# Two of four pairs of up chunks, in the second to fourth round of both MLPs, by seven products in place of eight

## Chip, cores and metric

The kernel runs on one core of one Trainium2 chip. The metric is the device time of one execution in microseconds (us). A core has the engines TensorE (PE; its weight loads are shown as PEld), VectorE (DVE), ScalarE (ACT) and GpSimd (POOL), and the queue SyncE (SP), which here issues the transfers.

## The reference

One inference step of a two-layer decoder over 512 prompt rows and 8 x 8 sample rows, 576 rows in all, with a model width of 1024. The change lies in the MLPs, one in each layer:

```python
def rmsnorm(x, g):
    y = x32 * lax.rsqrt(jnp.mean(x32 * x32, axis=-1, keepdims=True) + RMS_EPS)
    return (y * g.astype(jnp.float32)).astype(x.dtype)

def sqrelu_mlp(h, w_up, w_down):
    return jnp.square(jax.nn.relu(h @ w_up)) @ w_down

for l in range(DEPTH):
    ...
    hp = hp + sqrelu_mlp(rmsnorm(hp, norm_mlp[l]), mlp_w_up[l], mlp_w_down[l])
    hs = hs + sqrelu_mlp(rmsnorm(hs, norm_mlp[l]), mlp_w_up[l], mlp_w_down[l])
```

`w_up` is 1024 x 4096 and `w_down` 4096 x 1024, all in float32. The mixers (retention with gMLP, then attention) are not touched.

## The kernel before

Everything is held transposed: width on the 128 partitions, the 576 rows along the free axis, as two halves of 288 (`TH`). `h[0..7]` are the eight chunks of the residual stream. Each float32 product is made of three: both operands are split into a high part (`hi`, a cast on ACT) and a low part (`lo`, a subtraction on DVE), and PE adds hi x hi, hi x lo and lo x hi. For the norm's output these are `norm.xs[c]` (tiles xhi and xlo); for the weights they are `whi` and `wlo`, each 128 x 512, made in `prepare` (L272) and `split_low` (L283) with `NW_` = 6 buffers.

An MLP runs in four rounds of `rounds_of`. In a round, four pairs of **up chunks** come first. An up chunk (`up`, through `block`, L328) is 128 columns of `w_up`: eight blocks of the contraction, times three parts, times two halves, 48 products into one `acc` tile of two PSUM banks. Then DVE takes it out with relu and the norm's factor (tile `t`, L490), ACT squares it (tile `q`, L495), and once both chunks of a pair are there, four DVE passes over 288 columns (L503 to L506) make combinations, ACT casts them in two goes (`ahi`, L498) and DVE makes the low parts (`alo`, L499).

Four **down units** of `down_unit` follow. Each makes two row chunks and two halves from a 2 x 2 block product with seven products for eight (P1 to P7; L340 in `product`), where `q`'s combinations are the right operands, and combinations of weight blocks (`total`, L257: the sums s1 to s4, one DVE pass of 128 x 512 each) are among the left ones. Seven products of 12 matmuls stand in a unit. Results that take part in several outputs are carried on by ACT copies inside PSUM (`y`, `z`, `w`), between products that don't need them; in down units 1 to 3, P5 goes into a tile `f` of its own.

The order on DVE and ACT inside an MLP is the order of the code (`manual_schedule`). `jobs` lists which weight half or combination comes when; `ahead_to` prepares jobs some places ahead of PE, and `load_free` starts the transfer of the next `raw` weight tile (512 KB, three buffers; during the down units a fourth in the buffer of `q`) once a tile has been used up.

Of the kernel before, what the change touches and what calls it, by code (L numbers as in the profile page):

```python
# [11 lines left out]
F32 = mybir.dt.float32  # L12
F32R = mybir.dt.float32r
AF = mybir.ActivationFunctionType
ALU = mybir.AluOpType
# [3 lines left out]
P = 128  # L19
D = 1024  # L20
KC = D // P
NP = 512
NS = 64
T = NP + NS
TH = T // 2
# [5 lines left out]
FB = 8  # L31
# [10 lines left out]
NW_ = 6  # L42
# [70 lines left out]
NCOL = 59  # L113
UNIT = ("P1", "P5", "P6", "P2", "P7", "P3", "P4")
SUMS = {"P1": "s1", "P5": "s2", "P2": "s3", "P6": "s4"}
FIRST_UNIT = ("P1", "P2", "P3", "P5", "P6", "P4", "P7")


@with_exitstack
def hybrid_step(ctx: ExitStack, tc: tile.TileContext, a, o):  # L120
    nc = tc.nc
# [17 lines left out]
    def ks(name, dt=F32):  # L139
# [8 lines left out]
    cols = keep.tile([P, NCOL], F32, name="cols")  # L148
# [67 lines left out]
    used, done, summed = [0], [0], [0]  # L216
# [107 lines left out]
    def block(outs, w, x, sides, start, stop):  # L324

        for si, (w_, x_) in enumerate(((w[0], x[0]), (w[0], x[1]), (w[1], x[0]))):
            for hf, out in zip(sides, outs):
                nc.tensor.matmul(out, lhsT=w_, rhs=x_[:, hf if isinstance(hf, slice) else half(hf)],  # L328
                                 start=(start and si == 0), stop=(stop and si == 2))
# [13 lines left out]
    def cut(piece, k):  # L343
        return [w[:, (k % 4) * P:(k % 4 + 1) * P] for w in piece[k // 4]]
# [118 lines left out]

    def rounds_of(norm, nxt, mp):
        rounds, closing = 32 // FB, Closing(COL["fin"])

        def up():

            acc, got = acc_tile(), take(2)
            for k in range(KC):  # L470
                block([acc[:, hf, 0:TH] for hf in range(2)], cut(got, k), norm.xs[k], (0, 1), k == 0, k == KC - 1)
            ahead_to(used[0] + NW_ - 2)
            return acc[:, :, 0:TH]

        def flat(v):
            return v.rearrange("p a b -> p (a b)")

        for r in range(rounds):
            acts, firsts = [], []
            for p in range(FB // 2):  # L480

                q = mp.tile([P, 8, TH], F32, name="q", tag="q", bufs=1)
                hi = mp.tile([P, 7, TH], F32R, name="ahi", tag="ahi", bufs=FB // 2)
                lo = mp.tile([P, 7, TH], F32R, name="alo", tag="alo", bufs=FB // 2)
                for j in range(2):
# [4 lines left out]
                    nc.vector.scalar_tensor_tensor(out=halves(t), in0=view, scalar=0.0, in1=norm.rv,  # L490
                                                   op0=ALU.max, op1=ALU.mult)
                    if p == FB // 2 - 1 and j == 1:
                        ahead_to(used[0] + NW_ - 1)
                    seg = slice(2 * j, 2 * j + 2)
                    nc.scalar.activation(out=flat(q[:, seg]), in_=t, func=AF.Square)  # L495

                def two(s0, s1):
                    nc.scalar.copy(out=hi[:, s0 - 1:s1 - 1], in_=q[:, s0:s1])  # L498
                    nc.vector.tensor_tensor(out=lo[:, s0 - 1:s1 - 1], in0=q[:, s0:s1],  # L499
                                            in1=hi.bitcast(F32)[:, s0 - 1:s1 - 1], op=ALU.subtract)  # L500

                b12, b11, b22, b21, t1, t2, t3, t4 = (q[:, i] for i in range(8))
                nc.vector.tensor_tensor(out=t1, in0=b11, in1=b12, op=ALU.subtract)  # L503
                nc.vector.scalar_tensor_tensor(out=t2, in0=t1, scalar=-1.0, in1=b22, op0=ALU.mult, op1=ALU.subtract)
                nc.vector.tensor_tensor(out=t3, in0=b22, in1=b12, op=ALU.subtract)
                nc.vector.scalar_tensor_tensor(out=t4, in0=t2, scalar=-1.0, in1=b21, op0=ALU.mult, op1=ALU.subtract)  # L506
# [838 lines left out]
def layouts(i):  # L1345


    def chunks(w):

        r, c = w.shape  # L1350
        return w.reshape(r // P, P, c // P, P).transpose(2, 1, 0, 3)

    def down(w):

        return w.reshape(4, 4, 2, P, 4, 2, P).transpose(0, 4, 5, 3, 2, 1, 6).reshape(4, 4, 2, P, 8, P)

    def cols(v):
        return v.reshape(-1, P).T

    x = np.concatenate([i["x_prompt"][0], i["x_sample"].reshape(NS, D)])  # L1360
# [28 lines left out]
        "rot": ROT,  # L1389
    }  # L1390
    for l in range(2):
        out[f"w_up{l}"] = chunks(i["mlp_w_up"][l])
        out[f"w_dn{l}"] = down(i["mlp_w_down"][l])
    return {k: np.ascontiguousarray(v) for k, v in out.items()}


# [20 lines left out]
```

## Time and profile before

| what | value |
|---|---|
| median of 3 runs | 1208.14 us (1206.29 to 1211.4) |
| profiled execution's own time | 1207.19 us |
| its span, first to last instruction | 1205.4 us |
| mean granted clock of TensorE | 0.998 |
| HBM read and written | 102.92 MB and 6.03 MB |
| transfers of up weights | 64 of 512 KB |

The kernel runs mixer 0, MLP 0, mixer 1 and MLP 1. MLP 0's four rounds lie from about 257 us to 640, MLP 1's from about 811 to 1192, and one round takes some 95 us: about 50 for the up chunks, 45 for the down units. Where a line of the profile has a name such as `L328`, that is the line of the code above. "Busy" counts the time in which an engine works on something; a row of idle time names who ended it. The lines of the profile themselves stand in the prediction.

### The profile page before, as it was taken

The numbers are of one execution on the slowest core, as the hardware profiler recorded it, in microseconds if no ns is written. First come the engines' busy times: TensorE is split into PE (matmuls) and PEld (weight loads), VectorE is DVE, ScalarE is ACT, GpSimd is POOL, SyncE is SP. The second block draws the span as 40 slices with busy tenths as digits, with TensorE's granted clock in tenths as the row PEclk, the third lists the DMA queues.
The fourth block names the chain that finished last, engine by engine and source line by source line (L and its number), as shares of the span: only waits on it lengthen the run. The fifth ranks groups of instructions, "written<-read, shape, count | busy, mean of one in ns | idle before, by whom it ended". The sixth has DMA issues, their size and how long they took to land.

```text
span 1205.4 us, 22593 instructions
## 1 busy us (share of the span) xinstructions
PE 1186.1 (98%) x9177; PEld 1169.3 (97%) x9177; DVE 872.6 (72%) x1611; ACT 576.4 (48%) x1082; POOL 157.6 (13%) x137
## 2 busy tenths in 40 slices
PE   8999999999999999999999999999999999999996
PEld 8999999999999999999999999999999999999996
DVE  8977795447866875785797778546785795795696
ACT  6333554444443544453466777444453453453452
POOL 4444250110000000000002654220000000000000
PEclk9999999999999999999999999999999999999999
DMA  7343222222233232232223212122233232232222
GB/s 273 105 141 124 76 76 86 76 66 88 88 105 86 73 122 72 71 107 87 80 84 122 72 38 70 54 75 70 84 96 99 61 115 88 71 106 88 77 82 79
DMA packets 38263, 109.42 MB, mean 91 GB/s; under 512 B 4160, under 2 KB 12544, under 8 KB 38144
## 3 DMA queue, kind: packets, MB, share of 16 engines
q1 hardware_dynamic: 37440, 107.36, 28.8%
q8 instruction: 72, 1.18, 0.4%
q10 hardware_dynamic: 720, 0.62, 0.2%
q14 instruction: 31, 0.25, 0.1%
HBM read 102.92 MB, written 6.03 MB: 90 GB/s over the span
## 4 chain that ended last, share of the span: by engine, by line
PE 82%; DVE 10%; ACT 3%; DMA 3%; issue 2%; SPq 0%; DVEq 0%; ACTq 0%
PE acc L328 54%; PE acc L340 8%; PE f L340 3%; PE y L340 3%; PE w L340 3%; PE z L340 3%; DVE wlo L283 2%; DMA raw<-in_w_dn 2%; ACT s L1101 1%; PE tpp L1161 1%; DVE alo L499 1%; PE op L1176 1%; DVE h L547 1%; PE sp L1142 1%; ACT ahi L498 1%
## 5 line engine op out<-in xcount | busy, mean ns | idle before, releaser
L328 PE MATMUL acc<-xhi,whi 128*128 128x288 f32 x1504 | 321.4, 295 | 0.4 <-DVE vz L765 0.4
L328 PE MATMUL acc<-xhi,wlo 128*128 128x288 f32 x1504 | 319.0, 293 | 0.0
L328 PE MATMUL acc<-xlo,whi 128*128 128x288 f32 x1504 | 318.7, 293 | 0.0
L283 DVE TENSOR_TENSOR wlo<-raw,whi 128x512 fp32r<-128x512 f32 x321 | 232.2, 736 | 76.2 <-ACT whi L272 74.7
L272 ACT CAST whi<-raw 128x512 fp32r<-128x512 f32 x321 | 191.6, 618 | 133.7 <-PE acc L328 100.8
L328 PEld LDWEIGHTS acc<-xhi,whi 128*128 128x128 f32 x1504 | 239.3, 188 | 1.6 <-issue 1.2
L328 PEld LDWEIGHTS acc<-xhi,wlo 128*128 128x128 f32 x1504 | 240.4, 188 | 0.3
L328 PEld LDWEIGHTS acc<-xlo,whi 128*128 128x128 f32 x1504 | 240.0, 188 | 0.0
L495 ACT ACTIVATE q<-t 128x576 f32<-128x576 f32 x64 | 43.9, 686 | 229.5 <-DVE t L490 229.5
L490 DVE SCALAR_TENSOR_TENSOR t<-acc,rstd 128x576 f32<-128x576 f32 x64 | 48.3, 755 | 83.3 <-PE acc L328 82.7
L272 ACT CAST whi<-s 128x512 fp32r<-128x512 f32 x124 | 73.7, 620 | 64.7 <-DVE s L257 55.2
L283 DVE TENSOR_TENSOR wlo<-s,whi 128x512 fp32r<-128x512 f32 x124 | 84.1, 689 | 10.6 <-ACT whi L272 10.6
L499 DVE TENSOR_TENSOR alo<-q,ahi 128x864 fp32r<-128x864 f32 x64 | 77.1, 1205 | 8.3 <-ACT ahi L498 8.3
L498 ACT CAST ahi<-q 128x864 fp32r<-128x864 f32 x64 | 66.5, 1039 | 13.6 <-DVE q L506 12.6
L340 PE MATMUL acc<-ahi,wlo 128*128 128x288 f32 x340 | 71.4, 298 | 0.6
L340 PE MATMUL acc<-ahi,whi 128*128 128x288 f32 x340 | 71.4, 295 | 0.0
L340 PE MATMUL acc<-alo,whi 128*128 128x288 f32 x340 | 70.3, 295 | 0.0
L1046 POOL TENSOR_TENSOR kl<-z,kh 64x512 fp32r<-64x512 f32 x4 | 5.5, 1379 | 394.3 <-ACT kh L1043 394.1
L257 DVE TENSOR_TENSOR s<-raw 128x512 f32<-128x512 f32 x62 | 42.8, 690 | 18.7 <-DMA raw<-in_w_dn 18.7
L340 PEld LDWEIGHTS acc<-ahi,wlo 128*128 128x128 f32 x340 | 53.6, 188 | 2.5 <-DVE wlo L283 2.5
L340 PEld LDWEIGHTS acc<-ahi,whi 128*128 128x128 f32 x340 | 54.0, 188 | 0.0
L340 PEld LDWEIGHTS acc<-alo,whi 128*128 128x128 f32 x340 | 53.7, 188 | 0.0
(331 smaller groups left out, 2109.4 us busy)
## 6 DMA issues: line engine op xcount, KB each, us to landing
raw<-in_w_up SPq DMA_DIRECT2D x64, 512.0 KB
raw<-in_w_dn SPq DMA_DIRECT2D x64, 512.0 KB
raw<-in_w_in SPq DMA_DIRECT2D x22, 512.0 KB
raw<-in_w_o SPq DMA_DIRECT2D x16, 512.0 KB
raw<-in_w_qkv SPq DMA_DIRECT2D x10, 512.0 KB
h<-in_xT SPq DMA_DIRECT2D x8, 288.0 KB
s<-in_s SPq DMA_DIRECT2D x4, 512.0 KB
out_ret_s<-s SPq DMA_DIRECT2D x4, 512.0 KB
```

The costliest lines, as they stand in the source:

```text
L257: nc.vector.tensor_tensor(out=sums[k, i], in0=x, in1=b[y], op=ALU.add)
L272: nc.scalar.copy(out=hi, in_=src)
L283: nc.vector.tensor_tensor(out=lo, in0=src, in1=hi.bitcast(F32), op=ALU.subtract)
L328: nc.tensor.matmul(out, lhsT=w_, rhs=x_[:, hf if isinstance(hf, slice) else half(hf)], start=(start and si == 0), stop=(stop and si == 2))
L340: nc.tensor.matmul(out, lhsT=w[wi][:, k * P:(k + 1) * P], rhs=x(k)[xi], start=(start and n == 0), stop=(stop and n == len(steps) - 1), ski ...
L490: nc.vector.scalar_tensor_tensor(out=halves(t), in0=view, scalar=0.0, in1=norm.rv, op0=ALU.max, op1=ALU.mult)
L495: nc.scalar.activation(out=flat(q[:, seg]), in_=t, func=AF.Square)
L498: nc.scalar.copy(out=hi[:, s0 - 1:s1 - 1], in_=q[:, s0:s1])
L499: nc.vector.tensor_tensor(out=lo[:, s0 - 1:s1 - 1], in0=q[:, s0:s1], in1=hi.bitcast(F32)[:, s0 - 1:s1 - 1], op=ALU.subtract)
L547: nc.vector.tensor_tensor(out=row[:, cols_], in0=row[:, cols_], in1=src, op=op)
L1101: nc.scalar.activation(out=s[:, n, cut_:], in_=s[:, n, cut_:], func=AF.Exp, bias=nm[:, n:n + 1], accum_out=den[:, n:n + 1])
L1142: nc.tensor.matmul(sp[:, i * 256 + 256 - wd:(i + 1) * 256], lhsT=q[kv][:, n * P:(n + 1) * P], rhs=kst[kv][part][:, lo:lo + wd], start=(par ...
```

## The change

In rounds two to four (`r > 0`), the second and the fourth pair of up chunks (`p % 2 == 1`) are made by `up_unit`: a 2 x 2 block product over halves of the contraction, the two chunks, and the two halves of the rows, in seven products of 12 matmuls for eight. The other pairs stay as they are. This needs:

- combinations of the norm's operands (`mix`, called four times in the first round behind up chunks, the places in `MIX`): scaled sums and differences of `h` chunks, split in high and low parts (tiles `xn`), kept through the MLP;
- combinations of up weights, by the same `jobs` and `total` as the down units: four sums and seven splits where a pair had four splits;
- up weights laid out by pairs with the contraction's blocks in another order (`up` in `layouts`), which `up` in `rounds_of` follows;
- DVE writing its result to `q` at once (tile `t` is gone), which ACT squares in place;
- room in SBUF: the DMA scratch is set to 4096.

```diff
+    def in_units(r, p):
+
+        return r > 0 and p % 2 == 1
+
     def mlp_order(l, last):
...
-            add_pieces([up[r * FB + f] for f in range(FB)])
+            for p in range(FB // 2):
+                pair = [up[r * FB // 2 + p, i] for i in range(2)]
+                if in_units(r, p):
+                    add_unit(pair, False)
+                else:
+                    add_pieces(pair)
...
+        def mix(i):
+
+            a, b = 2 * i, 2 * i + 1
...
+            nc.scalar.activation(out=t3, in_=h[a][:, two_], func=AF.Copy, scale=ga)
+            for out, src, g, in1, op in ((t1, h[a][:, one], ga, t3, ALU.subtract), (t3, h[b][:, two_], gb, t3, ALU.subtract),
+                                         (u2, h[b][:, two_], gb, t1, ALU.add), (u4, h[b][:, one], gb, u2, ALU.subtract)):
+                nc.vector.scalar_tensor_tensor(out=out, in0=src, scalar=g, in1=in1, op0=ALU.mult, op1=op)
...
+            for src, sign, hi, lo in zip((t1, u2, t3, u4), (1, -1, 1, -1), his, los):
+                nc.scalar.activation(out=hi, in_=src, func=AF.Copy, scale=float(sign))
+                nc.vector.scalar_tensor_tensor(out=lo, in0=src, scalar=float(sign), in1=hi.bitcast(F32),
+                                               op0=ALU.mult, op1=ALU.subtract)
...
+        def up_unit(q):
+
+            both = acc_tile()
+            x, f = both[:, 0, 0:TH], both[:, 1, 0:TH]
+
+            def run(n, out, start, ahead=NW_ - 1):
+                product(out, take(1)[0], lambda k: [t[operand[n]] for t in mixed[k]], range(4), start, True, True)
+                if ahead:
+                    ahead_to(used[0] + ahead)
+
+            def copied(name, src):
+                out = m_tile(name)[:, 0:TH]
+                nc.scalar.copy(out=out, in_=src)
+                ahead_to(used[0] + NW_ - 1)
+                return out
+
+            def scaled(seg, src, op):
+                nc.vector.scalar_tensor_tensor(out=q[:, seg], in0=src, scalar=0.0, in1=norm.rv[:, seg % 2],
+                                               op0=op, op1=ALU.mult)
+
+            run("P1", x, True, 0)
+            y = copied("y", x)
+            run("P5", f, True)
+            run("P6", x, False, 0)
+            z = copied("z", x)
+
+            nc.scalar.copy(out=q[:, 3], in_=f)
+            run("P2", y, False)
+            scaled(1, y, ALU.max)
+            run("P7", z, False, 0)
+            w_ = copied("w", z)
+
+            nc.vector.tensor_tensor(out=q[:, 2], in0=z, in1=q[:, 3], op=ALU.add)
+            scaled(2, q[:, 2], ALU.min)
+            run("P3", x, False)
+            nc.vector.tensor_tensor(out=q[:, 0], in0=x, in1=q[:, 3], op=ALU.add)
+            scaled(0, q[:, 0], ALU.max)
+            nc.scalar.activation(out=flat(q[:, 0:2]), in_=flat(q[:, 0:2]), func=AF.Square)
+            run("P4", w_, False)
+            scaled(3, w_, ALU.min)
+            nc.scalar.activation(out=flat(q[:, 2:4]), in_=flat(q[:, 2:4]), func=AF.Square)
...
+                if in_units(r, p):
+                    up_unit(q)
+                for j in range(0 if in_units(r, p) else 2):
...
-                    t = mp.tile([P, T], F32, name="t", tag="t")
-                    nc.vector.scalar_tensor_tensor(out=halves(t), in0=view, scalar=0.0, in1=norm.rv,
+                    seg = slice(2 * j, 2 * j + 2)
+                    nc.vector.scalar_tensor_tensor(out=q[:, seg], in0=view, scalar=0.0, in1=norm.rv,
                                                    op0=ALU.max, op1=ALU.mult)
...
+                    if r == 0 and (p, j) in MIX:
+                        mix(MIX.index((p, j)))
```

Three places show how the order of instructions changes. Lines behind the change are some 10 higher up to `add_residual`, and more beyond.

**The second pair of the second round, on ACT and PE.** Before, ACT has behind a pair's second chunk its square (L495), the two casts of the pair (L498), two weight casts (L272) and the next chunk's square:

```order
L495 ACTIVATE q<-t 128x576 [waits DVE_49]
L498 CAST ahi<-q 128x864 [waits Activation_49]
L498 CAST ahi<-q 128x1152 [waits DVE_49]
L272 CAST whi<-raw 128x512 [waits DMAHW7_49,PE_49]
L272 CAST whi<-raw 128x512 [waits PE_49]
L495 ACTIVATE q<-t 128x576 [waits DVE_49,Activation_49]
```

With the change, the same first pair is followed on ACT by the copies of the unit (L525 is `copied`, L539 the copy of f to `q`):

```order
L576 ACTIVATE q<-q 128x576 [waits DVE_49]
L581 CAST ahi<-q 128x864 [waits Activation_49]
L581 CAST ahi<-q 128x1152 [waits DVE_49]
L525 COPY y<-acc 128x288 [waits PE_49]
L282 CAST whi<-s_4341 128x512
L282 CAST whi<-s_4284 128x512
L282 CAST whi<-raw 128x512 [waits DMAHW6_49]
L525 COPY z<-acc 128x288 [waits PE_49]
L282 CAST whi<-raw 128x512 [waits DMAHW7_49]
L539 COPY q<-acc 128x288 [waits DVE_49]
L282 CAST whi<-raw 128x512
L525 COPY w<-z 128x288 [waits PE_49]
```

The copy of y stands right behind the pair's two casts. On PE, the last rows of P1 and the first of P5 of that unit (P5's operand is a combination, `xn`; its result f lies in the same `acc` tile):

```order
L350 MATMUL acc<-xhi,whi 128x288
L350 MATMUL acc<-xhi,wlo 128x288
L350 MATMUL acc<-xlo,whi 128x288
L350 MATMUL acc<-xn,whi 128x288 [waits Activation_49]
L350 MATMUL acc<-xn,wlo 128x288
L350 MATMUL acc<-xn,whi 128x288 x2
```

P5's first matmul waits for ACT, for the count that the copy of y brings; P6 behind it has no wait for ACT of its own.

**The last pair of the second round, on DVE,** from the first chunk's evacuation, or what stands there, to the pair's last low part. Before (L490 takes a chunk out, s are sums of down weights):

```order
L490 SCALAR_TENSOR_TENSOR t<-acc,rstd 128x576
L283 TENSOR_TENSOR wlo<-s_4619,whi 128x512
L283 TENSOR_TENSOR wlo<-s_4536,whi 128x512
L490 SCALAR_TENSOR_TENSOR t<-acc,rstd 128x576
L283 TENSOR_TENSOR wlo<-s_4617,whi 128x512
L503 TENSOR_TENSOR q<-q 128x288
L504 SCALAR_TENSOR_TENSOR q<-q 128x288
L505 TENSOR_TENSOR q<-q 128x288
L506 SCALAR_TENSOR_TENSOR q<-q 128x288
L499 TENSOR_TENSOR alo<-q,ahi 128x864
L499 TENSOR_TENSOR alo<-q,ahi 128x1152
```

With the change, from the last sums of down weights on (L530 is `scaled`, L545 and L548 the additions of f; the four q passes and two alo follow as before):

```order
L267 TENSOR_TENSOR s_5853<-s_5808,raw 128x512
L267 TENSOR_TENSOR s_5855<-s_5853,raw 128x512
L530 SCALAR_TENSOR_TENSOR q<-y,rstd 128x288
L293 TENSOR_TENSOR wlo<-s_5855,whi 128x512
L545 TENSOR_TENSOR q<-z,q 128x288
L530 SCALAR_TENSOR_TENSOR q<-q,rstd 128x288
L293 TENSOR_TENSOR wlo<-s_5808,whi 128x512
L548 TENSOR_TENSOR q<-acc,q 128x288
L530 SCALAR_TENSOR_TENSOR q<-q,rstd 128x288
L293 TENSOR_TENSOR wlo<-s_5853,whi 128x512
L530 SCALAR_TENSOR_TENSOR q<-w,rstd 128x288
L586 TENSOR_TENSOR q<-q 128x288
```

The sums and low parts for the first down unit now stand among the unit's own passes, and ahead of these stand three low parts of the unit, two sums and two more low parts.

**The first pair of the first round, on DVE.** Before, behind the second chunk's evacuation:

```order
L490 SCALAR_TENSOR_TENSOR t<-acc,rstd 128x576
L503 TENSOR_TENSOR q<-q 128x288
L504 SCALAR_TENSOR_TENSOR q<-q 128x288
L505 TENSOR_TENSOR q<-q 128x288
L506 SCALAR_TENSOR_TENSOR q<-q 128x288
```

With the change (L498 and L505 are now lines of `mix`, L572 the evacuation, L586 the first q pass):

```order
L572 SCALAR_TENSOR_TENSOR q<-acc,rstd 128x576
L498 SCALAR_TENSOR_TENSOR x_3178<-h_74,cols,x_3179 128x288
L498 SCALAR_TENSOR_TENSOR x_3179<-h_78,cols,x_3179 128x288
L498 SCALAR_TENSOR_TENSOR x_3180<-h_78,cols,x_3178 128x288
L498 SCALAR_TENSOR_TENSOR x_3181<-h_78,cols,x_3180 128x288
L505 SCALAR_TENSOR_TENSOR xn<-x_3178,xn 128x288
L505 SCALAR_TENSOR_TENSOR xn<-x_3180,xn 128x288
L505 SCALAR_TENSOR_TENSOR xn<-x_3179,xn 128x288
L505 SCALAR_TENSOR_TENSOR xn<-x_3181,xn 128x288
L586 TENSOR_TENSOR q<-q 128x288
```

Eight passes have moved in between the evacuation and the pair's own.

More of the change, by code (lines that the diff above doesn't have):

```diff
@@ L465, in rounds_of @@
         rounds, closing = 32 // FB, Closing(COL["fin"])
+        operand = {"P1": 0, "P2": 2, "P3": 1, "P5": 3, "P6": 4, "P7": 5, "P4": 6}
+        mixed = []
         def up():
             acc, got = acc_tile(), take(2)
-            for k in range(KC):
-                block([acc[:, hf, 0:TH] for hf in range(2)], cut(got, k), norm.xs[k], (0, 1), k == 0, k == KC - 1)
+            for n, k in enumerate((0, 1, 2, 4, 5, 6, 3, 7)):
+                block([acc[:, hf, 0:TH] for hf in range(2)], cut(got, k), norm.xs[2 * (k % 4) + k // 4], (0, 1),
+                      n == 0, n == KC - 1)
@@ L472, in up @@
             ahead_to(used[0] + NW_ - 2)
             return acc[:, :, 0:TH]
+        def mix(i):
+            a, b = 2 * i, 2 * i + 1
+            ga, gb = (cols[:, norm.gcol + c:norm.gcol + c + 1] for c in (a, b))
+            one, two_ = slice(TH, T), slice(0, TH)
+            t1, t3, u2, u4 = (mp.tile([P, TH], F32, name=n, tag="sum", bufs=4) for n in ("x1", "x3", "x2", "x4"))
+            nc.scalar.activation(out=t3, in_=h[a][:, two_], func=AF.Copy, scale=ga)
+            for out, src, g, in1, op in ((t1, h[a][:, one], ga, t3, ALU.subtract), (t3, h[b][:, two_], gb, t3, ALU.subtract),
+                                         (u2, h[b][:, two_], gb, t1, ALU.add), (u4, h[b][:, one], gb, u2, ALU.subtract)):
+                nc.vector.scalar_tensor_tensor(out=out, in0=src, scalar=g, in1=in1, op0=ALU.mult, op1=op)
+            place = [ks("xn") for _ in range(4)] if i % 2 else [mp.tile([P, T], F32, name="xn", tag="xn", bufs=8)
+                                                                        for _ in range(4)]
+            place = [halves(t.bitcast(F32R))[:, j] for t in place for j in range(2)]
+            his, los = place[0:4], place[4:8]
+            for src, sign, hi, lo in zip((t1, u2, t3, u4), (1, -1, 1, -1), his, los):
+                nc.scalar.activation(out=hi, in_=src, func=AF.Copy, scale=float(sign))
+                nc.vector.scalar_tensor_tensor(out=lo, in0=src, scalar=float(sign), in1=hi.bitcast(F32),
+                                               op0=ALU.mult, op1=ALU.subtract)
+            parts_ = []
+            for part, mine in zip(range(2), (his, los)):
+                xa, xb = norm.xs[a][part], norm.xs[b][part]
+                parts_.append([xa[:, one], xb[:, two_], xb[:, one]] + mine)
+            mixed.append(parts_)
@@ L1391, in layouts @@
     for l in range(2):
-        out[f"w_up{l}"] = chunks(i["mlp_w_up"][l])
+        out[f"w_up{l}"] = up(i["mlp_w_up"][l])
         out[f"w_dn{l}"] = down(i["mlp_w_down"][l])
```

9 lines of the change are left out of this document (5 added, 4 removed).

## The prediction

> **What bounds the kernel now.** I read the page's busy line first, then the busy time by stage, then the chain that ended last in order of time, then DVE's and ACT's instructions in order of time at the seams between the up and the down chunks.
>
> ```profile
> PE 1186.1 (98%) x9177; PEld 1169.3 (97%) x9177; DVE 872.6 (72%) x1611; ACT 576.4 (48%) x1082; POOL 157.6 (13%) x137
> ...
> 402.50:447.70 45.20, 45.07 (x338) 44.60 (x337) 39.66 (x74) 22.87 (x42) 0.00 (x0) 1.00 0.31 96
> 447.70:497.60 49.90, 49.90 (x386) 49.90 (x386) 29.22 (x45) 19.45 (x29) 0.00 (x0) 1.00 0.28 83
> ...
> 413.00:424.00 11.00, 10.87 (x80) 10.57 (x80) 11.00 (x23) 5.80 (x13) 0.00 (x0) 1.00 0.31 85
> ```
>
> The columns of the windows are length, then the busy time of PE, PEld, DVE, ACT and POOL, the granted clock and the DMA share. TensorE (PE) sets the time in both MLPs. Up chunks leave DVE room (29.22 of 49.90 us), but down units do not: DVE is busy 11.00 of 11.00 us while PE still runs. The change takes work from PE and gives it to DVE.
>
> ```profile
> 436.52 1.59 PE acc L340 x12
> ...
> 446.10 1.59 PE w L340 x12
> 447.69 49.93 PE acc L328 x384
> ```
>
> These rows of the chain are start, length, work. Seven products of a down unit go from 436.52 to 447.69, 11.17 us. Four pairs of up chunks take 49.93 us, 12.48 a pair. An up pair made by seven products, as fast as those of the down unit and without a wait, saves 12.48 - 11.17 = 1.31 us; there are 2 x 3 x 2 = 12, so **15.7 us** is the most to gain.
>
> **What the change costs, one: a copy that PE waits for.** In a unit, P5 writes the second bank of the same acc tile from whose first bank ACT copies y, and the built order has P5's first product wait for ACT; up to P2 no other row of P6 does. ACT's copy stands behind both ahi casts of the pair before. When those end is in the trace:
>
> ```profile
> 390.01 0.76 DVE L490 SCALAR_TENSOR_TENSOR t<-acc,rstd 128x576 f32<-128x576 f32 x1 [1.14 <-PE acc L328]
> ...
> 391.59 0.46 DVE L504 SCALAR_TENSOR_TENSOR q<-q 128x288 f32<-128x288 f32 x1 [0.46 <-ACT q L495]
> ...
> 394.01 1.36 DVE L499 TENSOR_TENSOR alo<-q,ahi 128x1152 fp32r<-128x1152 f32 x1 [0.26 <-ACT ahi L498]
> ...
> 390.81 0.69 ACT L495 ACTIVATE q<-t 128x576 f32<-128x576 f32 x1 [4.29 <-DVE t L490]
> 391.52 0.92 ACT L498 CAST ahi<-q 128x864 fp32r<-128x864 f32 x1
> 392.82 1.16 ACT L498 CAST ahi<-q 128x1152 fp32r<-128x1152 f32 x1 [0.38 <-DVE q L506]
> 393.89 1.13 ACT L272 CAST whi<-raw 128x512 fp32r<-128x512 f32 x2
> ...
> 402.30 0.55 PE L340 MATMUL acc<-ahi,whi 128*128 128x288 f32 x3
> 402.49 0.76 DVE L490 SCALAR_TENSOR_TENSOR t<-acc,rstd 128x576 f32<-128x576 f32 x1 [0.69 <-PE acc L328]
> ...
> L583 ACT COPY y<-acc 128x288 f32<-128x288 f32 x3 | 1.1, 383 | 1.9 <-PE acc L340 1.8
> ```
>
> The evacuation starts 0.19 us after PE's next product (402.49 against 402.30). ACT is free of the second ahi cast 3.88 us after the evacuation began (393.89 - 390.01), a copy takes 0.38, and I add 0.05 for the signal. So P5 starts 4.5 us into the unit, where P1 ended at 11.17 / 7 = 1.6: PE waits **2.9 us**, and nothing hides it, since PE's queue is in order. The other copies (z, w, q3) have a product of 1.6 us between, and ACT's casts ahead of them take 0.52 to 0.6 each: no cost. The wait alone turns -1.31 into +1.6 us for each unit. The bounds: zero if the copy were done at P1's end, about 3.5 if DVE comes late to the evacuation.
>
> [...] The order names the wait at P5, so I take 2.9.
>
> **Two: DVE.** A unit adds three low parts and four sums of 128x512, and six passes of 288 take the place of two of 576. From start to start, DVE needs:
>
> ```profile
> 403.17 0.68 DVE L283 TENSOR_TENSOR wlo<-s,whi 128x512 fp32r<-128x512 f32 x1
> 403.77 0.45 DVE L503 TENSOR_TENSOR q<-q 128x288 f32<-128x288 f32 x1
> 404.32 0.46 DVE L504 SCALAR_TENSOR_TENSOR q<-q 128x288 f32<-128x288 f32 x1
> 404.70 0.45 DVE L505 TENSOR_TENSOR q<-q 128x288 f32<-128x288 f32 x1
> ...
> 405.44 1.05 DVE L499 TENSOR_TENSOR alo<-q,ahi 128x864 fp32r<-128x864 f32 x1
> 406.75 1.36 DVE L499 TENSOR_TENSOR alo<-q,ahi 128x1152 fp32r<-128x1152 f32 x1 [0.26 <-ACT ahi L498]
> 408.06 0.46 DVE L547 TENSOR_TENSOR h<-h,y 128x288 f32<-128x288 f32 x1
> ...
> 408.26 0.29 PE L340 MATMUL f<-ahi,whi 128*128 128x288 f32 x1
> ...
> 411.77 0.69 DVE L257 TENSOR_TENSOR s<-raw 128x512 f32<-128x512 f32 x1 [1.52 <-DMA raw<-in_w_dn]
> ```
>
> That is 0.60 for 512 columns (403.17 to 403.77), 0.37 for 288 (404.32 to 404.70), 0.68 for 576 (402.49 to 403.17), 1.31 and 1.3 for the two alo. So a unit adds 7 x 0.60 + 6 x 0.37 - 2 x 0.68 = 5.1 us of DVE, 61 us in all.
>
> In the first unit of a round this lies under PE: DVE came with slack, and 12.48 us of ordinary pair follow. A walk along DVE's order with these steps (low parts behind casts that ACT makes after its copies) has it about 0.5 us late at that pair's last evacuation. So the second unit's wait is 3.4 us and it ends 11.17 + 3.4 = 14.6 us after its start.
>
> At the seam to the down chunks there was no slack. Down unit 0 needs the last alo for its f product 5.96 us after it starts (402.30 to 408.26), and alo ended at 408.1. In the changed order, DVE has between the evacuation ahead of the second unit and its last alo: eight low parts, four sums (12 x 0.60), one pass of 576, fourteen of 288 (5.2), four alo (5.2), 18.3 us, from 0.7: 19.0 us if it never waits, against 14.6 + 6 = 20.6. But it does wait: for the square of each pair (0.46 at 391.59), for the second ahi, for casts that stand on ACT behind the square or the w copy (two of about 0.7), for products P3 and P4. The stops of my walk, in us from the second unit's start: evacuation 0.7; alo of the pair before 6.0; low parts of P7 and P3, s1, P4's low part, s3 by 9.0; two low parts of down unit 0, the second behind a cast after the q3 copy, 10.5; s2, s4, y's pass 12.2; the low part of s4, cast after the w copy, 13.1; z's passes and a low part 14.5; x's passes, open since P3's end at 12.9, 15.3; the last low part, cast behind the square, 17.2; w's pass 17.7; its square 18.4; the four q passes 19.6; second ahi 20.9; alo 22.3. So PE waits **1.5 to 1.7 us** more, at least zero; I take 1.5, as the waits are all in the order. After that DVE stands to PE as before: the next load (landed at 411.77, 3.6 us after alo) is tied to the same point.
>
> A round from the second on: 2.9 + 3.4 + 1.5 - 2.6 = **+5.2 us**, six of them +31.
>
> **Three: the first round.** Four mixes stand on DVE between evacuations, each eight passes of 288 (3.0 us, 3.2 with two dependent steps) behind ACT's scaled copy, which waits for the square: from the evacuation's 0.68 to 0.80 + 0.60 + 0.38, 1.1 us. That makes 4.3 each, 17.2 us a round. The room there, by its waits:
>
> ```profile
> L283 DVE TENSOR_TENSOR wlo<-raw,whi 128x512 fp32r<-128x512 f32 x13 | 8.5, 687 | 3.9 <-ACT whi L272 3.9
> L490 DVE SCALAR_TENSOR_TENSOR t<-acc,rstd 128x576 f32<-128x576 f32 x7 | 5.3, 755 | 3.5 <-PE acc L328 3.4
> L499 DVE TENSOR_TENSOR alo<-q,ahi 128x1152 fp32r<-128x1152 f32 x3 | 4.1, 1360 | 0.8 <-ACT ahi L498 0.8
> L257 DVE TENSOR_TENSOR s<-raw 128x512 f32<-128x512 f32 x2 | 1.4, 688 | 1.0 <-DMA raw<-in_w_dn 1.0
> L504 DVE SCALAR_TENSOR_TENSOR q<-q 128x288 f32<-128x288 f32 x3 | 1.4, 458 | 1.2 <-ACT q L495 1.2
> L283 DVE TENSOR_TENSOR wlo<-s,whi 128x512 fp32r<-128x512 f32 x2 | 1.3, 688 | 1.3 <-ACT whi L272 1.3
> ```
>
> 3.9 + 3.5 + 0.8 + 1.0 + 1.2 + 1.3 = 11.7 us. So DVE comes 5.5 us late to the seam; with only the bare 12 us of the mixes it would be 0.3. PE feels it first where the fourth pair wants an acc buffer that isn't evacuated, and then at the seam. I take 6 us in each MLP (0 to 7), as no other room is in the order: **+12**.
>
> **At nothing:** the up weights' new layout (64 loads of 512 KB as before), the changed order of the eight blocks (same products), t gone (its passes remain), ACT's 2.8 us more a unit (ACT is busy 19.45 of 49.90), the smaller DMA scratch (only hardware queues appear). If the raw tiles come late, DVE waits some tenths, which is in the walk.
>
> **The sum** is made against the profiled execution, 1207.2 us with a span of 1205.4, 0.9 below the median: 1207.2 + 31 + 12 = **1250**.
>
> **Rivals.** (a) Only the copies cost, DVE's lateness hides in PE's own waits: 12 x 2.9 - 15.7 = +19, 1226. For it: the bare sum of 19.0 us is under 20.6. Against: DVE's waits on ACT. 17%. (b) On the other side: ACT's copy is ready at P1's end, or P5 doesn't wait; one mechanism, decided by whether y is copied by 1.6 us into the unit. Then 15.7 us come through where DVE keeps up: 1191. Against it stands 393.89 - 390.01. 4%. [...] 4%. (d) The waits are long enough for the clock to fall. The end of the kernel shows it:
>
> ```profile
> 1195.00:1196.00 1.00, 0.04 (x1) 0.00 (x0) 1.00 (x4) 0.27 (x1) 0.00 (x0) 1.00 0.85 300
> 1196.00:1197.00 1.00, 0.75 (x2) 0.30 (x2) 0.49 (x2) 0.17 (x1) 0.00 (x0) 1.00 0.73 258
> 1197.00:1198.00 1.00, 0.00 (x0) 0.00 (x0) 0.45 (x1) 0.50 (x1) 0.00 (x0) 1.00 0.78 278
> 1198.00:1199.00 1.00, 0.00 (x0) 0.00 (x0) 0.92 (x3) 0.00 (x0) 0.00 (x0) 1.00 0.00 0
> 1199.00:1200.00 1.00, 0.00 (x0) 0.00 (x0) 0.97 (x3) 0.00 (x0) 0.00 (x0) 0.76 0.00 0
> ```
>
> PE did 0.8 us of work after 1195, and the clock went from 1.00 to 0.50 at about 1199.5, 4.5 us later. Waits of 2.9 to 3.4 us between products are shorter. If each halved the clock for as long as it lasted, 12 x 1.5 = 18 us: 1268. [...] 8%.
>
> **How the numbers follow.** The forecast has 64%, the rest 3%. The range runs from (a) with 2 us to spare, 1224, to (d), 1268. Slower by over 0.5% (about what a measurement of this kernel can tell from no change): 93%; within 0.5%: 3%; faster: 4%.
>
> **What would show it.** In the changed profile PE should wait for ACT's y at the second product of each unit, some 3 us, 12 times; up rounds two to four should last 49.9 + 3.7 us; DVE should be busy nearly throughout the second unit; f of down unit 0 should wait for alo; the first round should be some 3 us longer. If P5 starts at once, step one is wrong; if round one is 49.9 us and its seam clean, step three is.

## The result, and the profile after

| | before | after |
|---|---|---|
| median of 4 runs | 1208.01 us (1206.29 to 1211.4) | 1283.86 us (1277.33 to 1287.79) |
| profiled execution's own time | 1207.19 us | 1287.79 us |
| its span | 1205.4 us | 1286.0 us |
| mean granted clock of TensorE | 0.998 | 0.972 |

The changed kernel takes **1.0622** times as long, 95% interval 1.0601 to 1.0643. The sign was forecast, the size was not: 1250, with a range up to 1268. The profiled execution after the change is the slowest of its four.

The page's busy line and its row of the granted clock, after:

```profile
PE 1207.3 (94%) x9033; PEld 1183.0 (92%) x9033; DVE 962.5 (75%) x1807; ACT 629.0 (49%) x1206; POOL 157.4 (12%) x137
...
PEclk9999999999998999999899999998999998998899
```

There are 144 products fewer than before (9177), yet PE is busy for 21 us longer (1186.1 before). A slower PE would do that, and the row of clocks has eights in it; by itself it is no proof, since the busy time grows with the waits too (the run with 12 idle products below, at a clock of 0.992, has 9177 products as before and 1206.1 us). The waits of PE, by who ended them (us in total, times, longest):

```profile
PE acc L350 <- ACT y L525: 35.5, 12, 3.9
PE acc L338 <- DVE q L572: 7.8, 2, 4.1
PE acc L350 <- DVE wlo L293: 6.4, 8, 1.1
PE acc L350 <- DVE alo L582: 5.4, 8, 0.9
PE acc L350 <- ACT ahi L581: 3.7, 7, 0.9
```

These are the terms of the forecast by name: the copy of y twelve times, the first rounds (q, two times) and the seam, where an up round passes to its down units (wlo, alo, ahi). They add up to 58.8 us; less the gain of 15.7 that is 43, what the prediction's sum had, if otherwise made up. Yet the kernel is 76 us slower. The windows show in which stages the rest lies. After: first round's up chunks, its down units, the second round's up chunks, its down units, MLP 1's last up chunks (length, busy PE, PEld, DVE, ACT, POOL, clock, DMA share, GB/s):

```profile
256.80:313.70 56.90, 52.76 (x391) 52.41 (x390) 44.56 (x81) 29.16 (x51) 1.43 (x1) 0.97 0.19 56
313.70:362.50 48.80, 45.90 (x338) 44.69 (x337) 41.30 (x77) 25.14 (x46) 0.00 (x0) 1.00 0.33 98
362.50:419.00 56.50, 50.76 (x362) 50.29 (x361) 39.48 (x67) 24.29 (x41) 0.00 (x0) 0.94 0.24 71
419.00:466.50 47.50, 45.70 (x339) 44.72 (x338) 40.08 (x77) 24.10 (x44) 0.00 (x0) 1.00 0.30 94
1164.30:1224.60 60.30, 53.43 (x363) 52.96 (x362) 40.54 (x70) 25.29 (x44) 0.00 (x0) 0.89 0.21 67
```

And the first round before:

```profile
256.80:307.40 50.60, 50.60 (x390) 50.60 (x389) 33.77 (x52) 23.64 (x35) 1.43 (x1) 1.00 0.24 74
307.40:352.40 45.00, 44.92 (x339) 44.68 (x338) 39.66 (x74) 22.86 (x42) 0.00 (x0) 1.00 0.32 96
```

Up rounds with units were to last 53.6 us. They last 56.5 to 60.3, and it is there and in the first rounds that the clock is under 1. How that comes about shows on PE at the two units of the second round, in order of time (start, length; in brackets the idle time ahead and who ended it):

```profile
376.45 0.29 PE L350 MATMUL acc<-xlo,whi 128*128 128x288 f32 x1
379.42 0.40 PE L350 MATMUL acc<-xn,whi 128*128 128x288 f32 x1 [2.68 <-ACT y L525]
379.66 0.29 PE L350 MATMUL acc<-xn,wlo 128*128 128x288 f32 x1
...
406.69 0.61 PE L350 MATMUL acc<-xn,whi 128*128 128x288 f32 x1 [3.06 <-ACT y L525]
407.10 0.44 PE L350 MATMUL acc<-xn,wlo 128*128 128x288 f32 x1
407.34 0.68 PE L350 MATMUL acc<-xn,whi 128*128 128x288 f32 x2
```

Both waits are near the forecast (2.9 and 3.4). A wait costs more than its row says: the row counts from the modelled end of the product before, 0.29 us after its start, where products otherwise start 0.13 apart, and 0.24 pass behind the first one. From 376.45 to 379.66 are 3.21 us, less two steps of 0.13 is 2.95: some 0.25 more than 2.68. But behind the second the products stand 0.24 us apart in place of 0.13. Windows of 3.41 us around both waits, with the clock third from the end of the row:

```profile
375.13:378.54 3.41, 1.61 (x13) 1.37 (x11) 2.98 (x6) 2.22 (x3) 0.00 (x0) 1.00 0.01 5
378.54:381.95 3.41, 2.53 (x19) 2.53 (x20) 3.16 (x5) 2.43 (x5) 0.00 (x0) 1.00 0.02 5
...
402.44:405.85 3.41, 1.19 (x9) 0.95 (x8) 3.02 (x7) 2.26 (x3) 0.00 (x0) 1.00 0.46 154
405.85:409.26 3.41, 2.57 (x11) 2.57 (x12) 3.16 (x5) 2.38 (x5) 0.00 (x0) 0.50 0.00 0
409.26:412.68 3.42, 3.42 (x16) 3.42 (x16) 1.48 (x3) 0.00 (x0) 0.00 (x0) 0.50 0.40 108
412.68:416.09 3.41, 3.41 (x27) 3.41 (x27) 2.13 (x4) 1.80 (x5) 0.00 (x0) 1.00 0.11 46
```

In 402.44 to 405.85 PE worked for 1.19 of 3.41 us, and the next 3.41 us have half the clock; in these it idled for another 0.84, and a second slow stretch follows; PE never waits in that one, and the clock is back behind it. The wait of 2.68 us at 376.74 fell across a boundary, 1.80 us on one side and 0.88 on the other, and the clock stayed. The slow stretches all start on one grid of 3.413 us, and sum to 71 us of this execution, against 5.9 before (the kernel's end alone).

### The profile page after: what moved, and what is told of

It is laid out like the page before. It is cut to its first block, busy times and chain, and to the rows that moved or that the text cites. A ratio compares the mean times of both kernels' runs of the same rounds, so it can differ in the third digit from the quotient of the medians.

```text
span 1286.0 us, 22605 instructions
## 1 busy us (share of the span) xinstructions
PE 1207.3 (94%) x9033; PEld 1183.0 (92%) x9033; DVE 962.5 (75%) x1807; ACT 629.0 (49%) x1206; POOL 157.4 (12%) x137
## 4 chain that ended last, share of the span: by engine, by line
PE 56%; DVE 23%; ACT 11%; DMA 5%; issue 4%; SPq 0%; POOL 0%; DVEq 0%; ACTq 0%; POOLq 0%
PE acc L338 26%; PE acc L350 13%; DVE wlo L293 6%; ACT ahi L581 3%; PE f L350 3%; PE y L350 3%; PE w L350 3%; PE z L350 3%; ACT whi L282 2%; DMA raw<-in_w_dn 2%; DVE q L572 2%; DVE alo L582 2%; DMA raw<-in_w_up 2%; ACT q L576 2%; DVE s L267 1%
## 5 line engine op out<-in xcount | busy, mean ns | idle before, releaser
L338 PE MATMUL acc<-xhi,whi 128*128 128x288 f32 x1120 | 243.4, 299 | 8.2 <-DVE q L572 7.8
L338 PE MATMUL acc<-xhi,wlo 128*128 128x288 f32 x1120 | 241.0, 297 | 0.0
L338 PE MATMUL acc<-xlo,whi 128*128 128x288 f32 x1120 | 240.7, 297 | 0.0
L338 PEld LDWEIGHTS acc<-xhi,whi 128*128 128x128 f32 x1120 | 180.6, 190 | 10.0 <-issue 9.4
L338 PEld LDWEIGHTS acc<-xhi,wlo 128*128 128x128 f32 x1120 | 182.1, 190 | 0.3
L338 PEld LDWEIGHTS acc<-xlo,whi 128*128 128x128 f32 x1120 | 181.4, 190 | 0.0
L293 DVE TENSOR_TENSOR wlo<-s,whi 128x512 fp32r<-128x512 f32 x172 | 117.5, 694 | 20.5 <-ACT whi L282 20.5
L350 PE MATMUL acc<-xn,whi 128*128 128x288 f32 x192 | 59.6, 398 | 35.5 <-ACT y L525 35.5
L350 PEld LDWEIGHTS acc<-xn,whi 128*128 128x128 f32 x192 | 47.0, 279 | 38.3 <-ACT y L525 38.3
L581 ACT CAST ahi<-q 128x864 fp32r<-128x864 f32 x64 | 66.2, 1035 | 17.2 <-DVE q L589 16.3
L267 DVE TENSOR_TENSOR s<-s,raw 128x512 f32<-128x512 f32 x86 | 59.5, 692 | 0.3
```

What stands on the lines that cost most here:

```text
L267: nc.vector.tensor_tensor(out=sums[k, i], in0=x, in1=b[y], op=ALU.add)
L293: nc.vector.tensor_tensor(out=lo, in0=src, in1=hi.bitcast(F32), op=ALU.subtract)
L350: nc.tensor.matmul(out, lhsT=w[wi][:, k * P:(k + 1) * P], rhs=x(k)[xi], start=(start and n == 0), stop=(stop and n == len(steps) - 1), ski ...
```

## The experiments

Each was timed beside the kernel before, 1207.2 to 1207.7 us in these sets.

**Filling the waits.** If the clock answers PE's idle time, idle work in the same place must bring it back, and leave everything else.

```diff
+            w1 = parts[used[0]]
             run("P1", x, True, 0)
+            dm = m_tile("dm")[:, 0:TH]
+            for _ in range(21):
+                nc.tensor.matmul(dm, lhsT=w1[0][:, 0:P], rhs=mixed[0][0][0], start=True, stop=True)
             y = copied("y", x)
```

> Computes what the changed kernel does, with 252 products more: in each of the twelve units 21 idle products of 128x288 go to a spare PSUM tile behind the unit's first product, about 21 x 0.133 = 2.8 us of work in the place where PE waits for ACT's copy of y. Nothing that the chain y waits for is moved. Theory A (the time of the changed kernel is its waits as forecast, 1250 us, and behind them some 33 us of half clock that these waits set off): the copies come as late as before, PE's waits for y fall from 35.5 us in all to about 1 to 8 us, the stretches at half clock in the up rounds go, the granted clock is 0.99 or more, and the time is 1250 to 1256 us. Theory B (the units cost what they do by themselves, by ACT and DVE behind PE, and the lower clock is only a mark of it): 1280 to 1290 us. Theory C (the clock falls for what the units compute, not for PE's idle time): the clock stays at 0.97 to 0.98 and the time at 1280 us or more.

Measured: **1268.62** (ratio 1.0507, 1.049 to 1.0525). The waits of PE in it:

```profile
PE acc L350 <- ACT y L525: 2.3, 5, 0.9
```

No stretch in an up round with units is slow any more, clock 0.995. A kernel with 252 products more is faster by 15 us, so the clock had a price of its own (theories B and C fall). But 1268.6 is above A's 1256: at full clock, too, something costs more than the forecast had. The next runs find where.

The same with 12 products in place of 21 (`range(12)`):

> The changed kernel with 12 idle products of 128x288 (about 1.6 us) behind each unit's first product, in place of the 21 that left no wait. What is left of PE's waits for y should be 1.1 us in a first unit and 1.5 us in a second. Theory A (in the traces so far the clock halves for 3.41 us when PE has waited more than about 1.8 us within one stretch of a fixed grid of 3.41 us): no unit has a wait long enough, the up rounds keep the full clock, and the time is that of the kernel with 21 products, 1262 to 1270 us. Theory B (the clock falls in proportion to the waiting, or at any wait on this copy): half of the stretches stay, and the time lies between, 1274 to 1280 us.

Measured: **1266.99** (1.05, 1.0482 to 1.0517). Theory A. The waits, then the second round's two stages:

```profile
PE acc L350 <- ACT y L525: 16.3, 12, 2.2
```

```profile
362.60:416.40 53.80, 51.34 (x387) 50.87 (x386) 39.67 (x67) 24.25 (x41) 0.00 (x0) 1.00 0.26 76
416.40:464.00 47.60, 45.71 (x338) 44.73 (x338) 39.62 (x76) 24.02 (x44) 0.00 (x0) 1.00 0.30 93
```

Eleven waits of 1.1 to 1.6 us kept the clock; the twelfth, of 2.18 us, fell into one stretch of the grid and cost 3.4 us at half. This is the cleanest cut: 16.3 us of waits and 144 products of 0.133 us, 19.2, (twelve take 1.6 us) make 35.5 us, just the changed kernel's waits. So both kernels lose the same time to the copies, and their difference, 1283.86 - 1266.99 = **16.9 us, is the clock**, nearly all of it in the units: the two profiled executions are 21 us apart, and 19 of these lie in the six up rounds with units. The up round takes 53.8 us, forecast 53.6.

With 6 products:

> The changed kernel with 6 idle products (0.8 us) behind each unit's first product; PE's waits for y should be left at about 1.9 us in a first unit and 2.3 us in a second, 26 us in all. Theory A (the clock halves for the next stretch of a fixed 3.41-us grid where PE has waited over about 1.8 us within one stretch): whether a wait does it hangs on where it lies in the grid; a wait of length W puts over 1.8 us into one stretch with a chance of (3.41 + W - 3.6) / 3.41, 0.5 for 1.9 us and 0.62 for 2.3, so 5 to 9 of the twelve units are followed by a stretch at half clock, and the time lies between the kernel with 12 idle products (1267) and the changed kernel (1284): 1272 to 1280 us. Theory B (only a wait of about 2.7 us or more does it, wherever it lies): none or one, 1265 to 1270 us.

Measured: **1272.39** (1.0541, 1.0525 to 1.0557). Waits of 1.89 to 2.72 us; four of twelve were followed by a slow stretch, fewer than the five to nine that I expected, but the four are those with 1.89 us or more inside one stretch of the grid (1.89, 2.00, 2.05, 2.18), and the other eight have at most 1.77. Theory A in kind, B falls.

**Undoing parts.** First the mixes alone, with no pair made by units:

```diff
-        return r > 0 and p % 2 == 1
+        return False
```

> Computes what the kernel before does, since no pair goes by units; only the first round's part of the change stays: the norm's combinations made once, with their copies and casts, and kept. By the forecast this part costs 2 x 6 = 12 us of the total: 1220 us, and up to 7 us more where the clock falls once in the first round of each MLP (a stretch of 3.4 us at half clock costs 1.7 us). If the mixes hide beside the products: 1208 to 1212 us. If this part is where most of the 76 us are lost: 1250 us or more.

Measured: **1227.15** (1.0161, 1.0145 to 1.0176), the upper end of the first case. First round, its down units, and the second round's down units:

```profile
257.00:314.90 57.90, 53.76 (x391) 53.42 (x390) 45.59 (x82) 29.09 (x51) 1.42 (x1) 0.94 0.18 55
314.90:362.80 47.90, 45.58 (x337) 44.60 (x337) 41.06 (x77) 25.07 (x46) 0.00 (x0) 1.00 0.34 100
412.70:458.00 45.30, 45.08 (x338) 44.61 (x337) 39.66 (x74) 22.85 (x42) 0.00 (x0) 1.00 0.32 95
```

DVE has 45.59 us of work in 57.90, against 33.77 in 50.60. The round is 7.3 us longer, of which 4.14 is one wait of PE for an acc buffer that DVE hasn't emptied:

```profile
299.75 0.82 PE L338 MATMUL acc<-xhi,whi 128*128 128x288 f32 x2 [4.14 <-DVE q L572]
```

That wait sets off 6.8 us at half clock, and so does its like in MLP 1. The seam behind gives 2.9 us more (47.90 against 45.00); later rounds are as before, so what else this kernel keeps of the change (the layout of the up weights, the missing t, the smaller scratch) costs nothing there.

Then the units alone: the combinations are left out, and the units read parts of the plain operands, so that the results are not those of the step.

```diff
-            t1, t3, u2, u4 = (mp.tile(...) ...)
...
+            his, los = ([norm.xs[c][part][:, s] for c in (a, b) for s in (one, two_)] for part in range(2))
```

> Leaves the norm's combinations out: the units read quarters of the operands' own high and low halves in their place, so that the first round does no more work than before the change, and the units do the same products, copies and passes. Theory A (the parts add up): the changed kernel's 1284 less the 19.5 us that the mixes alone cost, 1260 to 1268 us, the first round and its down phase as before the change (50.6 and 44.9 us), the waits for y 33 to 37 us. Theory B (the units are late because the mixes' data or DVE's lateness of the first round carries on): the waits for y fall by a third or more, and the time is under 1255 us.

Measured: **1265.87** (1.0496, 1.0469 to 1.0524), with a first round of 50.6 us, as before the change, and these waits for y:

```profile
PE acc L350 <- ACT y L512: 35.8, 12, 4.0
```

Theory A, the parts add up: 58 us here and 19.5 with the mixes alone make 78, and the change has 76.

**The seam to the down units.** In the filled kernel with 21 products, the weight splits issued behind a unit's last product go behind the pair's casts:

```diff
-            run("P4", w_, False)
+            run("P4", w_, False, 0)
...
                 two(4, 8)
+                if in_units(r, p):
+                    ahead_to(used[0] + NW_ - 1)
```

> The kernel with 21 idle products, and one more edit: the weight splits that a unit's last product issues are put behind the pair's casts, so that DVE's last pass of the unit doesn't stand behind a low half that waits for ACT's square. That wait and the low half take 1.26 + 0.6 = 1.9 us at each seam to a down phase. Theory A (the down phases are 2.3 us longer for this lateness on DVE): the down phases behind units fall to 45.5 to 46 us, and the time is 6 x 1.9 = 11 us below that of 21 products alone, 1254 to 1261 us. Theory B (they are longer for the weights' low halves that the down unit itself waits for): 1265 to 1271 us.

Measured: **1252.93** (1.0384, 1.0369 to 1.04), 15.7 us below the filled kernel. The second round's two stages:

```profile
362.60:416.10 53.50, 53.50 (x405) 53.25 (x404) 39.49 (x67) 24.16 (x41) 0.00 (x0) 1.00 0.24 75
416.10:461.90 45.80, 45.38 (x338) 44.64 (x338) 39.51 (x76) 23.87 (x44) 0.00 (x0) 1.00 0.32 97
```

The down units go from 47.6 us to 45.8, near the 45.2 of before. What stood in the way is on DVE in the changed kernel:

```profile
421.61 0.69 DVE L293 TENSOR_TENSOR wlo<-s,whi 128x512 fp32r<-128x512 f32 x1 [1.26 <-ACT whi L282]
422.22 0.45 DVE L530 SCALAR_TENSOR_TENSOR q<-w,rstd 128x288 f32<-128x288 f32 x1
```

DVE waits 1.26 us for a weight's cast that ACT makes behind its square, and only then scales w, some 3 us behind the end of its product. PE's waits at this seam in the changed kernel, two in the first down unit and one in the next, are these; in the run the first two are gone, and the third is under 0.4 us (1.1 in the last round, as in the changed kernel):

```profile
424.39 0.40 PE L350 MATMUL acc<-ahi,whi 128*128 128x288 f32 x1 [0.47 <-ACT ahi L581]
...
425.65 0.41 PE L350 MATMUL acc<-alo,whi 128*128 128x288 f32 x1 [0.59 <-DVE alo L582]
...
434.03 0.81 PE L350 MATMUL acc<-ahi,wlo 128*128 128x288 f32 x4 [0.73 <-DVE wlo L293]
```

Theory A, a little below its range. Of the 13.1 us between the two profiled executions, 10.5 lie in the six down phases (1.6 to 2 each), near the 11 expected, and 2.5 in the up rounds.

**The place of the waits.** f in a PSUM tile of its own:

```diff
-            x, f = both[:, 0, 0:TH], both[:, 1, 0:TH]
+            x, f = both[:, 0, 0:TH], m_tile("f")[:, 0:TH]
```

> Same computation. f gets a PSUM tile of its own instead of the second half of x's tile, so the second product no longer waits for the copy of y, and only the third does, some 1.3 us later. Theory A (waits first, clock behind them): PE's waits for y fall from 35.5 us to about 12 x 1.6 = 19 us, each of them too short for the clock to fall, so that most of the half clock in the up rounds goes too: 1228 to 1245 us. If the clock falls at any wait that ends behind the same late copy, whatever its length: 1284 - 16 = 1268 us. If the tile made no difference to the second product's wait (it waits for the copy itself): 1280 to 1288 us.

Measured: **1258.82** (1.0422, 1.0407 to 1.0438). P5 no longer waits, P6 does:

```profile
PE acc L350 <- ACT y L525: 21.0, 12, 3.0
```

It is 1.1 us in the first units (1.4 in the last round), 1.8 to 3.0 in the second. The second half of my expectation failed, and the time is above its 1245: four of the longer waits still set off slow stretches, and two more slow stretches follow the waits at the seam, where ahi alone is waited for 1.3 us in these rounds. All slow stretches make 41 us of the execution, the kernel's end left out and the first rounds' among them.

The copy of y issued ahead of the pair's q passes and casts (these go into a function that the unit calls behind the copy):

```diff
-            y = copied("y", x)
+            y = m_tile("y")[:, 0:TH]
+            nc.scalar.copy(out=y, in_=x)
+            before()
```

> Same computation. The four passes over q and the two casts to ahi and alo of the pair before a unit are issued behind the unit's copy of y instead of ahead of it, so that on ACT the copy no longer stands behind both casts. Theory A (the wait is the place of the copy in ACT's row): PE's waits for y fall from 35.5 us to under 8 us, the clock is 0.99 or more in the up rounds, and what is left of the cost is the first rounds' mixes and DVE, which is busy through most of the unit and ends later at the seam to the down phase: 1222 to 1240 us. Theory B (the copy waits for the square or for x itself, and the casts only fill the time): the waits stay at 30 us or more and the time at 1275 us or more.

Measured: **1255.08** (1.0394, 1.0378 to 1.0409); the waits for y fall from 35.5 to 15.3 us, so the casts were what the copy stood behind, but the time is 15 us above what I expected. ACT and PE in the second unit of the second round:

```profile
402.31 0.68 ACT L582 ACTIVATE q<-q 128x576 f32<-128x576 f32 x1 [1.51 <-DVE q L578]
402.90 0.39 ACT L535 COPY y<-acc 128x288 f32<-128x288 f32 x1
```

```profile
403.35 0.40 PE L350 MATMUL acc<-xn,whi 128*128 128x288 f32 x1 [1.92 <-ACT y L535]
```

Here the copy stands behind ACT's square, and that waits for DVE, which comes late from the unit's sums and low parts. This wait of 1.92 us lies inside one stretch, and the next one, from 403.92 on, ran at a clock of 0.50.

Then all at once: that square too, f apart, the splits of the last product behind the casts.

> Computes what the changed kernel does. All that made units wait is moved: the square, the q passes and the casts of the pair before a unit stand behind the copy of y, f has its own PSUM tile, and the splits of a unit's last product stand behind the casts. The first rounds' mixes stay as in the changed kernel. Theory A (the units gain 12 x 1.31 = 15.7 us once nothing waits, and the clock falls only in the two first rounds): the time of the mixes alone, 1227, less 15.7 and up to 5 us of small waits left: 1211 to 1217 us; PE's waits for y under 5 us in all. Theory B (DVE cannot follow seven products in the up rounds wherever its passes stand): the waits come back behind q, ahi or alo, 15 us or more of them, and the time is 1225 us or more.

Measured: **1247.89** (1.0338, 1.0322 to 1.0353). Theory B. The waits of PE that take the place of those for y:

```profile
PE z L350 <- ACT z L525: 12.5, 12, 1.9
PE acc L350 <- ACT ahi L588: 8.8, 8, 1.2
PE acc L338 <- DVE q L578: 7.8, 2, 4.1
PE acc L350 <- DVE alo L589: 5.4, 8, 0.9
```

The up rounds are down to 50 us (the last to 51), which is no gain on the 49.9 of before, and the down units behind them take 48.4 in place of 45.2: what is put off ahead of the second unit comes due at its end, where DVE is already late. At the seam the waits of 1.22 us for ahi and 0.59 for alo, together 1.81, set off a slow stretch in five of six rounds.

Last, the low halves of the mixes on GpSimd, in that kernel:

```diff
-                nc.vector.scalar_tensor_tensor(out=lo, in0=src, scalar=float(sign), in1=hi.bitcast(F32), ...)
+                split_into(src, hi, lo, nc.gpsimd)
```

> As the kernel before it in this set, and the low halves of the first round's combinations are made by GpSimd instead of DVE (4 x 4 passes of 128x288, 4 x 1.56 us off DVE in each first round). Theory A (PE waits 4.1 and 3.7 us in the first rounds since DVE has too much work there): these waits fall below 1.5 us, the clock stays up there, and the time is about 2 x 5.5 = 11 us below that kernel's, 1198 to 1206 us, below the kernel before the change. Theory B (GpSimd's passes hold up DVE's, or come late for the first unit): no more than 3 us are gained, 1209 us or more.

Measured: **1259.52** (1.0434, 1.042 to 1.045), 12 us slower than without: Theory B. GpSimd and DVE in the first round:

```profile
292.67 4.06 POOL L231 TENSOR_TENSOR xn<-x,xn 128x288 fp32r<-128x288 f32 x4 [3.52 <-ACT xn L230]
```

```profile
294.02 1.06 DVE L599 TENSOR_TENSOR q<-q 128x288 f32<-128x288 f32 x1
295.12 0.95 DVE L600 SCALAR_TENSOR_TENSOR q<-q 128x288 f32<-128x288 f32 x1
295.99 1.05 DVE L601 TENSOR_TENSOR q<-q 128x288 f32<-128x288 f32 x1
296.97 0.45 DVE L602 SCALAR_TENSOR_TENSOR q<-q 128x288 f32<-128x288 f32 x1
```

While GpSimd works, DVE's passes of 288 take about 1 us in place of 0.45; from its end at 296.73 on they take 0.45 again. PE's longest waits in the first rounds grow from 4.1 and 3.7 us to 4.9 in both, and most of the 12 us lie there and in the down units behind. No version tried beats the kernel before: the mixes alone cost 19.5 us, more than the 15.7 that twelve units can gain.

## Why the prediction was right or wrong, point by point

- **What bounds the kernel.** Right, but for the clock: the cost is where DVE and ACT stand in PE's way. That DVE has no room at the seam, or for the mixes, was read from the profile of before and held.
- **One: the copy that PE waits for.** Right in place and size: twelve waits, 2.68 us in a first unit and 3.06 in the second (3.0 and 3.9 in the last round). In each of the twelve, P5 started 0.05 us behind the end of the copy (379.42 against 378.98 + 0.39), what the forecast had put in for the signal, and PE started nothing else in the wait (no product between 376.45 and 379.42). Counted from product to product, as the forecast did, at full clock the first unit lasts 14.09 us in place of 11.17, 2.9 more, and the second, in the run with 12 idle products, 14.39, 3.2 more; forecast 2.9 and 3.4. Up rounds at full clock took 53.8 us, forecast 53.6. That the casts ahead of the copy cause most of it is shown by putting the copy ahead of them (35.5 us of waits fall to 15.3). Rival (b), without a wait at P5, falls, and so does any other in which only P6 waits. With f in a tile of its own P5 did start at once (376.53 us, 0.14 behind P1's last product), and P6 waited 1.1 us in first units.
- **Two: the seam.** Right in kind, too small: 1.5 us forecast, 47.6 - 45.2 = 2.4 measured. PE waits there 0.5 for ahi, 0.6 for alo and 0.7 for a weight's low half, 1.8 by the rows, and each wait costs some 0.25 more; my walk had the low half behind the square in it as a delay on DVE but no wait of PE for low parts later. The sign that I named, f waiting for alo, was at the wrong product: PE waits at acc's products with the last pair, ahead of f's. Six seams: 14.4 us in place of 9. Rival (a), in which this lateness hides, falls.
- **Three: the mixes.** 12 forecast, 19.5 measured alone. PE does wait for the acc buffer and then at the seam, as put; the excess is mostly the half clock behind the two waits of 4.1 and 3.7 us, each with 6.8 us at half speed in the run with the mixes alone (less PE's idle time in these, and halved, 5.4 us for both: an estimate).
- **The step that failed: rival (d), the clock.** I held it for an alternative of 8%, to be had in place of the forecast, where it belonged in the sum. The argument against it was the kernel's end: the clock fell 4.5 us after PE's last long work, and waits of 2.9 to 3.4 us "are shorter". But those 4.5 us were no limit on a wait. By the grid of that trace the fall came at 1199.52, at the end of the stretch from 1196.10 on, the first in which PE was mostly idle (0.75 us of work, against 2.35 in the stretch before); over the runs, stretches with 1.89 us or more of idle time were followed by a slow one 57 times of 57. Its price, 18 us, is near the measured 16.9 by chance, for it came another way: the clock doesn't fall for as long as the wait lasts, but for one or two stretches of 3.41 us behind it. What made the range miss is that (d) came on top of the full waits, and that its 1268 left nothing for the seam and the mixes being short as well: 1250 + 17 + 5 + 7.5 is 1280 by itself.

The account, from the kernel before at 1207.2: units' waits less gain 6 x 3.9 = 23.4 (22.2 forecast), seams 14.4 (9), mixes with their clock 19.5 (12), 2.5 more in the last round of the run with 12 products, which has a slow stretch and lasts 56.4 us; that is its 1267.0; the clock in the units 16.9 (0); together 1283.9. Of the 34 us that the forecast lacks, the clock has some 17 in the units and, by the estimate above, 5 in the first rounds.

## What to carry to other kernels

A wait of some 2 us on the matmul engine, otherwise full, cost more than 2 us here: where 1.89 us or more of one 3.41-us stretch lay idle, the next one or two ran at half the clock, up to 1.7 or 3.4 us on top. So look where a wait falls among the stretches of the trace. A cheap way out was to fill part of the wait with idle products: a dozen, 1.6 us, saved 16.9 / 12 = 1.4 us a unit. Removing products didn't pay here: ACT and DVE, which feed the next ones, made PE wait 58.8 us, against 15.7 to gain. And a single weight split between two passes made 1.8 of the 2.4 us of lateness at a seam (47.6, 45.8 without it, 45.2 before).

## What the runs showed of the hardware

**The clock went by a fixed grid.** In each trace every slow stretch started at the same remainder of 3.413 us (3.07 in the changed kernel, 14 times), and its clock was 0.50, against 1.00 in the others. Over all twelve kernels' traces from 200 us on, PE's idle time within one full-clock stretch of the grid, summed from the rows of waits, goes with the clock of the next: in 57 of 57 stretches with 1.89 us or more the next one ran at half clock; in 127 with 0.8 to 1.64 us none did; between 1.65 and 1.85 us, 14 did and 9 did not. (The last 10 us of each kernel, where PE runs out of work, are left out.) Several short waits counted together (1.22 + 0.59). Within a slow stretch less idleness kept the next one slow: 0.8 us or more did in 16 of 16. Four falls, all in the second mixer, had no wait in the rows; they stay unexplained. The length of a wait alone didn't settle it: one of 1.92 us inside one stretch was followed by half the clock (the copy issued first), and one of 2.68 us across two stretches, 1.80 and 0.88, was not (the changed kernel).

**The same program, other times.** The changed kernel spreads over 10 us (1277.33 to 1287.79) where the kernel before spreads over 5, and its times go with the granted clock (0.983 in the fastest execution, 0.972 in the slowest). That the waits fall otherwise into the grid in each execution would explain it; it isn't shown, as only one execution of each kernel was traced.

**Passes of DVE took longer beside GpSimd's.** In the run with the low halves on GpSimd, the passes from q to q, 128x288 in SBUF, took 0.95 to 1.06 us beside GpSimd's (1.02 us each), and 0.45 without.
